# A state-space layer's tables moved from GpSimd to VectorE, its recurrence regrouped into two equal chains, its state products cut into quarter tiles

## The chip, the core and the metric

The program runs on one core of one Trainium2 chip. The core has five engines with a queue each: TensorE (PE in the profile; its weight loads are PEld), VectorE (DVE), ScalarE (ACT), GpSimd (POOL) and SyncE (SP, which here only issues DMAs). The engines run side by side and wait for each other by semaphores; a queue is worked off in order, so that an instruction that waits holds up all behind it. The metric is the device time of one execution in microseconds (us), lower is better.

## What is computed

A two-layer model on 256 tokens of width 2048, all in 32-bit floats. Layer 0 is a complex diagonal state-space mixer (S5: 128 groups of 16 channels with 64 complex states each) with a gated linear unit (GLU), then a SwiGLU feed-forward block; layer 1 is dilated-window attention and a second feed-forward block. The change is in the mixer alone:

```python
lb = exp(lam * dt)                         # complex, 128 x 64
bb = ((lb - 1) / lam) * b                  # 128 x 64 x 16
h[t] = lb * h[t-1] + bb @ u[t]             # 256 tokens, by groups
y[t] = real(c @ h[t]) + d_skip * u[t]
g = gelu(y);  val, gate = split(g @ w_glu) # 2048 x 4096
x = x + val * sigmoid(gate)
```

## The kernel before

**The mixer in blocks of four tokens.** The 256 tokens are 64 blocks of four. With the powers of `lb` up to the fourth (`pf1` to `pf4`, made by `power`), a block's input to the state is a sum of four tap matrices (`taps`, tile `gp`), the state from block to block is a recurrence with `pf4`, and the output of a block is a local product within the block (`y_local`, with the matrices `mt`) plus a product of the state with powers times `c` (`y_state`, with the tables `fd`, made by `powers`). Partitions hold two groups of 64 states; the 64 group pairs are cut into four quarters `qr` of 16. One half (32 pairs) shares an input tile `ub` and a state tile `st`.

**A quarter's steps.** `gain` scales `b` (one product); `taps` are six pairs of a 128x512 product (`gpr`) and a 128x256 sum; `taps_T` transposes them on TensorE in four groups, each copied by ScalarE to `gt`; `inject` multiplies them with the inputs in four groups, each copied by ScalarE into the state tile (two copies). `build_c` makes `cp` (two pairs of product and sum), `build_m` multiplies the taps with masked copies of `cp` (`cb`) on TensorE, and `store_m`, `finish_m` and six small DMAs make `mt` of it. `powers` are eight more pairs of product and sum. `spread` makes masked copies `fbd` of `fd` on ScalarE, 16 instructions a quarter.

**Who does what.** VectorE makes the parameters, the first quarter's taps, `build_c` of two quarters and the recurrence; GpSimd makes `gain`, the other taps, the other `build_c`, all `powers` and `finish_m`. `InOrder` (T, A, G, W for TensorE, ScalarE, GpSimd, VectorE) keeps these instructions in the order of the code; nearly all carry the line of its helper (L65), so the rows are read by tile names. Small tables (`NA`, `NP`, `NC`, `NH_`, ...) say how many steps of the recurrence go between other work.

**The recurrence** is 63 steps of three VectorE instructions: a product (tile `spr`), a sum (`ssm`), and an addition into the state (tile `actr`, the shared name of all big activation tiles). Before it is cut into chains `a` (quarter 0), `b` (quarters 1 and 2) and `c` (quarter 3), and steps of two chains alternate.

**The GLU** follows quarter by quarter: `y_state`, then Gelu (`gm`), four transposes for each half of the quarter (`y_T`), a hi copy by ScalarE and a lo difference by VectorE (`actt`), and then the weights' products. Each weight chunk (1 MB, four rows of 128) is split in two halves into `whi` (ScalarE) and `wlo` (VectorE); a row of weights gives six matmuls of 128x512. The first gate and the first value block, 16 rows of weights each, are fed side by side, as soon as a quarter of the mixer's output is there; the other six of the eight blocks follow (`block`, lines 128 to 130). After the GLU the kernel is such blocks to its end.

```python
def run(n, *its):
    for _ in range(n):
        for it in its:
            op = next(it, None)
            ...
order = [(blk, nb, c) for c in range(4) for blk, nb in ((0, 4), (1, 0))]
```

Of the kernel before, what the change touches and what calls it, by code (L numbers as in the profile page):

```python
# [15 lines left out]
ALU = mybir.AluOpType  # L16
# [31 lines left out]
NP = 39  # L48
NL = 0
NC = 7  # L50
NG_ = (6, 8, 11, 15)
NA = 54
NY = 11
NH_ = ((15, 11, 11, 18), (12, 12, 12, 12), (15, 15, 27, 15), (0, 0, 0, 0))
SPN = (6, 6, 4, 0)
# [12 lines left out]
class Net:  # L68
# [141 lines left out]
    def s5_glu(self):  # L210
# [8 lines left out]
        nc.sync.dma_start(out=spp, in_=io["sp"])  # L219
        pairs = early.tile([P, P], FP32, name="pairs")  # L220
        nc.sync.dma_start(out=pairs, in_=io["pairs"])
        for q in range(2):
            nc.sync.dma_start(out=xc[:, 16 * q:16 * q + 16], in_=io["x_c"][:, 16 * q:16 * q + 16])
        masks = late.tile([P, 2], FP32, name="masks")
        nc.sync.dma_start(out=masks, in_=io["masks"])
        nc.sync.dma_start(out=self.ident, in_=io["ident"])

# [35 lines left out]
        state = {0: (sts[0], 0), 1: (sts[1], 0), 2: (sts[1], 16), 3: (sts[0], 16)}  # L263

        gps = {}
        def gain(qr):
            bt = early.tile([P, 2, 16, GI], FP32, name="bt", tag="bt", bufs=1)
            nc.sync.dma_start(out=bt, in_=io["b"][:, :, 16 * qr:16 * qr + 16])
            gb = early.tile([P, 16, GI], FP32, name="gb", bufs=2)
            nc.sync.dma_start(out=gb, in_=io["gain_b"][:, 16 * qr:16 * qr + 16])  # L270
            if qr < 2:
                g = early.tile([P, 2, 16, 4, GI], FP32, name="gp", tag="gp", bufs=2)
            else:
                g = self.xres.tile([P, 2, 16, 4, GI], FP32, name="gp", tag="xr")
            tt(g[:, :, :, 3], bt, gb.unsqueeze(1).broadcast_to([P, 2, 16, GI]), ALU.mult, G)
            gps[qr] = g

        def c_load(qr):
            ct = late.tile([P, 2, 16, GI], FP32, name="ct", tag="fd", bufs=4)
            nc.sync.dma_start(out=ct, in_=io["c"][:, :, 16 * qr:16 * qr + 16])  # L280
            return ct

        gain(0)
        cts = {qr: c_load(qr) for qr in range(4)}
        ds = late.tile([P, 2, 64], FP32, name="ds")
        dmask = late.tile([P, GI], FP32, name="dmask")
        nc.sync.dma_start(out=ds, in_=io["dsk"])
        nc.sync.dma_start(out=dmask, in_=io["dmask"])
# [44 lines left out]
        def form(nm, z, eng=V):  # L333
            f = late.tile([P, 2, 2, 64], FP32, name=nm)
            eng.tensor_copy(out=f[:, 0, 0], in_=z[:, 0])
            eng.tensor_copy(out=f[:, 1, 1], in_=z[:, 0])
            eng.tensor_copy(out=f[:, 1, 0], in_=z[:, 1])
            eng.tensor_scalar(out=f[:, 0, 1], in0=z[:, 1], scalar1=-1.0, scalar2=None, op0=ALU.mult)
            return f

        def cmul(out, f, z, eng=V):
            pr = early.tile([P, 2, 2, 64], FP32, name="pr", tag="gprv", bufs=1)
            tt(pr, f, z.unsqueeze(1).broadcast_to([P, 2, 2, 64]), ALU.mult, eng)
            tt(out, pr[:, :, 0], pr[:, :, 1], ALU.add, eng)

        pf = [form("pf1", lam, W)]
# [4 lines left out]
        def power(eng=V):  # L351
            k = len(pf) + 1
            z = early.tile([P, 2, 64], FP32, name=f"pw{k}")
            cmul(z, pf[0], pw[-1], eng)
            pw.append(z)
            pf.append(form(f"pf{k}", z, eng))

        power(W)
        power(W)
# [19 lines left out]
        gts = {}  # L379

        def taps(qr, eng, nm):
# [125 lines left out]
        def run(n, *its):  # L507
            for _ in range(n):
                for it in its:
                    op = next(it, None)  # L510
                    if op is not None:
                        op()
# [494 lines left out]
```

## Time and profile before

| | us |
|---|---|
| median of 3 runs (2507.66 to 2507.81) | 2507.7 |
| profiled execution, first to last instruction | 2504.1 |
| TensorE busy | 2391.9 |
| VectorE busy | 1411.4 |
| ScalarE busy | 1106.7 |
| GpSimd busy | 162.4 |
| two of eight GLU blocks done at | 253.9 |

Times in the trace are counted from its first instruction; the time of a run has 3.6 us more than the profiled span (2507.7 less 2504.1). Busy time of TensorE tells little in the first 250 us, because its matmuls are short there and overlap; what matters is when it waits, and for whom.

### The profile page before, as it was taken

The numbers are of one execution on the slowest core, as the hardware profiler recorded it, in microseconds if no ns is written. First come the engines' busy times: TensorE is split into PE (matmuls) and PEld (weight loads), VectorE is DVE, ScalarE is ACT, GpSimd is POOL, SyncE is SP. The second block draws the span as 40 slices with busy tenths as digits, with TensorE's granted clock in tenths as the row PEclk, the third lists the DMA queues.
The fourth block names the chain that finished last, engine by engine and source line by source line (L and its number), as shares of the span: only waits on it lengthen the run. The fifth ranks groups of instructions, "written<-read, shape, count | busy, mean of one in ns | idle before, by whom it ended". The sixth has DMA issues, their size and how long they took to land.

```text
span 2504.1 us, 28310 instructions
## 1 busy us (share of the span) xinstructions
PE 2391.9 (96%) x11200; PEld 1935.8 (77%) x11200; DVE 1411.4 (56%) x2098; ACT 1106.7 (44%) x1423; POOL 162.4 (6%) x156
## 2 busy tenths in 40 slices
PE   5439999999999999999999999999999999999999
PEld 5427888888888888888888888878888888888887
DVE  9997545445444444555545667765444444454444
ACT  6316444444433444445444555545444433344433
POOL 7911000000000000000000100100000000000000
PEclk8569999999999999999999999999999999999999
DMA  3103555555555555555555444445555555555554
GB/s 115 63 1 120 185 186 185 184 186 183 185 187 189 186 185 181 182 185 194 185 185 172 165 154 149 152 151 178 180 185 182 185 185 190 192 185 179 186 194 148
DMA packets 64949, 423.50 MB, mean 169 GB/s; under 512 B 8240, under 2 KB 12208, under 8 KB 14384
## 3 DMA queue, kind: packets, MB, share of 16 engines
q1 hardware_dynamic: 63664, 419.60, 49.2%
q8 instruction: 87, 1.43, 0.2%
q10 hardware_dynamic: 1152, 2.10, 0.2%
q14 instruction: 46, 0.38, 0.0%
HBM read 418.79 MB, written 2.10 MB: 168 GB/s over the span
## 4 chain that ended last, share of the span: by engine, by line
PE 91%; DVE 8%; issue 0%; ACT 0%; POOL 0%; DMA 0%; POOLq 0%
PE mm L128 29%; PE mm L130 29%; PE mm L129 29%; DVE actr L65 2%; DVE spra L65 1%; DVE ssma L65 1%; PE mm L65 1%; PE ms L847 1%; PE tr L733 1%; DVE sprb L65 1%; PE tr L798 1%; DVE ssmb L65 1%; DVE sprc L65 1%; DVE gpr L65 0%; PE tr L847 0%; PE tr L191 0%
## 5 line engine op out<-in xcount | busy, mean ns | idle before, releaser
L110 DVE TENSOR_TENSOR wlo<-raw,whi 128x1024 fp32r<-128x1024 f32 x768 | 939.2, 1225 | 991.6 <-ACT whi L109 990.2
L109 ACT CAST whi<-raw 128x1024 fp32r<-128x1024 f32 x768 | 804.6, 1048 | 1147.8 <-PE mm L130 1130.5
L128 PE MATMUL mm<-whi,actt 128*128 128x512 f32 x3072 | 1221.3, 398 | 1.1 <-ACT whi L109 1.1
L130 PE MATMUL mm<-whi,actt 128*128 128x512 f32 x3072 | 1215.0, 396 | 0.0
L129 PE MATMUL mm<-wlo,actt 128*128 128x512 f32 x3072 | 1214.8, 395 | 0.0
L130 PEld LDWEIGHTS mm<-whi,actt 128*128 128x128 f32 x3072 | 575.9, 187 | 138.6
L128 PEld LDWEIGHTS mm<-whi,actt 128*128 128x128 f32 x3072 | 576.0, 188 | 137.7 <-ACT whi L109 1.6
L129 PEld LDWEIGHTS mm<-wlo,actt 128*128 128x128 f32 x3072 | 576.0, 187 | 136.6
L65 PE MATMUL mm<-fbd,actr 128*64 128x128 f32 x64 | 6.3, 382 | 66.5 <-DVE actr L65 66.5
L180 POOL TENSOR_TENSOR r<-m,mhalf 128x1 f32<-128x1 f32 x6 | 3.2, 552 | 995.0 <-DVE m L179 848.9
L785 POOL TENSOR_TENSOR sc<-ssq,mhalf 128x8 f32<-128x8 f32 x16 | 32.1, 2005 | 475.0 <-DVE ssq L783 475.0
L65 PEld LDWEIGHTS mm<-fbd,actr 128*64 128x64 f32 x64 | 6.2, 233 | 66.6 <-issue 66.6
L65 PE MATMUL mm<-whi,actt 128*128 128x512 f32 x128 | 47.0, 435 | 7.2 <-DVE actt L65 6.9
L719 ACT ACTIVATE sg<-mm,r 128x512 f32<-128x512 f32 x44 | 30.1, 689 | 21.3 <-PE mm L130 21.1
L65 PEld LDWEIGHTS mm<-whi,actt 128*128 128x128 f32 x128 | 25.8, 204 | 14.9 <-DVE actt L65 8.3
L856 ACT ACTIVATE s<-s,mx 128x384 f32<-128x384 f32 (+1 forms) x32 | 24.8, 774 | 25.2 <-DVE mx L854 25.2
L65 POOL TENSOR_TENSOR fpr<-pf,cp 128x512 f32<-128x512 f32 x32 | 34.6, 1080 | 2.3
L65 ACT ACTIVATE gm<-mm 128x512 f32<-128x512 f32 x2 | 1.2, 598 | 70.0 <-PE mm L65 70.0
L723 DVE SCALAR_TENSOR_TENSOR sg<-mm,r,sg 128x512 f32<-128x512 f32 x44 | 30.9, 744 | 0.0
L65 DVE TENSOR_TENSOR spra<-pf,actr 128x64 f32<-128x64 f32 x63 | 30.4, 482 | 0.6
L65 DVE TENSOR_TENSOR ssma<-spra 128x32 f32<-128x32 f32 x63 | 29.3, 465 | 0.5
L781 ACT ACTIVATE sq<-mm 128x512 f32<-128x512 f32 x32 | 19.0, 593 | 23.5 <-PE mm L130 23.5
(190 smaller groups left out, 1243.7 us busy)
## 6 DMA issues: line engine op xcount, KB each, us to landing
raw<-w_gu SPq DMA_DIRECT2D x176, 1024.0 KB, 4.8
raw<-w_down SPq DMA_DIRECT2D x88, 1024.0 KB, 4.9
raw<-w_q SPq DMA_DIRECT2D x48, 1024.0 KB, 4.9
raw<-w_kv SPq DMA_DIRECT2D x32, 1024.0 KB, 4.9
raw<-w_glu SPq DMA_DIRECT2D x30, 1024.0 KB, 4.9
raw<-w_o SPq DMA_DIRECT2D x16, 1024.0 KB, 4.9
actr<-x_c SPq DMA_DIRECT2D x2, 1024.0 KB, 6.1
actr<-w_glu SPq DMA_DIRECT2D x2, 1024.0 KB, 7.1
```

What stands on the lines that cost most here:

```text
L65: return lambda *a, **k: self.tc.keep_in_program_order(call(*a, **k))
L109: (scalar or self.nc.scalar).copy(out=hi, in_=r)
L110: (vector or self.nc.vector).tensor_tensor(out=lo, in0=r, in1=hi.bitcast(FP32), op=ALU.subtract)
L128: matmul(ps[th], lhsT=a[:, 0, ts], rhs=hi, start=(k == 0), stop=False)
L129: matmul(ps[th], lhsT=a[:, 0, ts], rhs=lo, start=False, stop=False)
L130: matmul(ps[th], lhsT=a[:, 1, ts], rhs=hi, start=False, stop=(k == n - 1))
L719: nc.scalar.activation(out=s, in_=ps[th], func=AF.Silu, scale=rs[th])
L723: nc.vector.scalar_tensor_tensor(out=sg[th], in0=ps[th], scalar=rs[th], in1=sg[th], op0=ALU.mult, op1=ALU.mult)
L733: nc.tensor.transpose(out=pt[:, k, th * P:(th + 1) * P], in_=sg[th][:, c:c + P], identity=self.ident)
L785: nc.gpsimd.tensor_tensor(out=sc, in0=ssq, in1=self.mhalf.rearrange("p (a b) -> p a b", a=2), op=ALU.pow)
L798: nc.tensor.transpose(out=pt[:, hh, th * P:(th + 1) * P], in_=ns[th][:, 2 * hp + hh], identity=self.ident)
L847: nc.tensor.matmul(pss[g], lhsT=q[g][:, th * P:(th + 1) * P], rhs=kT[:, h, 0:n], start=True, stop=True)
```

## The change

Everything lies in the function of layer 0.

- VectorE makes all tables: `gain`, `taps`, `build_c` and `powers` of all quarters. GpSimd keeps the memsets, one product `dsm` (128x1024) at the start and the power for the norm.
- `taps_T` and `inject` become one function, `taps_inject`: a group's transposes, its copy, its products and its copies stand behind each other before the next group's.
- `store_m` adds `dsm` on VectorE; the copy on ScalarE and GpSimd's addition go.
- The tables stand ahead of the recurrence, which is two chains of equal width (32 pairs each), run alternately to their end with nothing between. The small tables of numbers go.
- `spread` goes. `y_state` reads `fd` itself in quarter tiles: 64 rows by 64 columns of the array, 64 matmuls of 64 columns a quarter instead of 32 of 128.
- In the GLU only the first gate block is fed beside the mixer's output; the first value block is an ordinary block behind it. The early load of the first two weight chunks goes; all weight splits' differences are on VectorE (four of 16 halves were on GpSimd).
- `b`, `gain_b` and `c` are loaded whole at the start.

```diff
-        def taps(qr, eng, nm):
+        def pair(out, f, src):
+            pr = early.tile([P, 2, 16, GI], FP32, name="gpr", bufs=2)
+            yield lambda: tt(pr, f.unsqueeze(3).broadcast_to([P, 2, 16, GI]), src, ALU.mult, W)
+            yield lambda: tt(out, pr[:, 0], pr[:, 1], ALU.add, W)
+
+        def taps(qr):
             mo = 16 * qr
             g = gps[qr]
...
-        def taps_T(qr):
-            g = gps[qr]
-            gts[qr] = []
+        def taps_inject(qr):
+            g, st, mo = gps[qr], sts[qr // 2], 16 * (qr % 2)
             for j2 in range(4):
                 gtt = early.tile([P, 2, 2, P], FP32, name="gt", tag="gt", bufs=4)
-                gts[qr].append(gtt)
                 ps = self.ps_tr.tile([P, 2, 2, P], FP32, name="tr")
...
                 A.copy(out=gtt, in_=ps)
-
-        def inject(qr):
-            st, mo = state[qr]
-            for j2 in range(4):
                 ps = self.ps_mm.tile([P, 2, 2, 2, NS], FP32, name="mm")
...
-                A.copy(out=mt[r, 3, mo:mo + 16].rearrange("p (j y) o -> p j y o", y=2), in_=ps[r, :, :, xx])
...
+                tt(mt[r, 3, mo:mo + 16].rearrange("p (j y) o -> p j y o", y=2), ps[r, :, :, xx],
+                   dsm[r, mo:mo + 16].rearrange("p (j y) o -> p j y o", y=2), ALU.add, W)
...
-        def y_state(qr, j4, ps):
-            st, mo = state[qr]
-            for j in range(4):
+        def y_state(qr, pss):
+            st, mo = sts[qr // 2], 16 * (qr % 2)
+            for jq in range(8):
                 for ri in range(2):
                     for xx in range(2):
-                        mq = 2 * (4 * j4 + j) + xx
-                        T.matmul(ps[64 * xx:64 * xx + 64, j],
-                                 lhsT=st[:, 0:64, ri, mo + mq],
-                                 rhs=fb[qr][j4][:, :, ri, :, mq - 8 * j4].rearrange("p y t o -> p t y o"),
-                                 start=False, stop=(ri == 1), skip_group_check=True)
...
+                        for y in range(2):
+                            r = slice(64 * y, 64 * y + 64)
+                            T.matmul(pss[y][64 * xx:64 * xx + 64, jq],
+                                     lhsT=st[r, 0:64, ri, mo + 2 * jq + xx],
+                                     rhs=fds[qr][r, :, ri, 2 * jq + xx],
+                                     start=False, stop=(ri == 1), skip_group_check=True)
...
+        run(taps(0))
+        taps_inject(0)
+        power()
         gain(2)
-        taps(2, G, "g")
...
+        gain(3)
+        run(taps(1), coefs())
+        taps_inject(1)
         build_u(1)
...
+        run(taps(2))
+        taps_inject(2)
+        run(taps(3))
+        taps_inject(3)
+        fd = self.act_raw([P, 2, 4, 2, 16, GI])
+        fds = {0: fd[:, 0], 1: fd[:, 1]}
+        run(*[build_c(qr) for qr in range(2)])
+        run(*[build_c(qr) for qr in range(2, 4)])
         ms = {}
         for qr in range(4):
...
+            ms[qr] = build_m(qr)
+            if qr > 1:
+                fds[qr] = self.xres.tile([P, 4, 2, 16, GI], FP32, name="fdx", tag="xr")
+            run(powers(qr))
             if qr:
                 store_m(qr - 1, ms[qr - 1])
...
+        run(scan("a", 0), scan("b", 1))
...
+        prepare(0)
+        y_state(0, yl[0])
+        gms = {0: gelu(yl[0])}
+        y_state(1, yl[1])
...
+        y_T(0, gms[0])
+        gms[1] = gelu(yl[1])
+        gb0 = self.open_block(KT)
+        for c in range(4):
+            if c + 1 < 4:
+                prepare(c + 1)
+            for w in ws.pop(c):
+                self.products(gb0, w, lhs, T)
+            if c < 2:
+                yl[c + 2] = y_local(c + 2, self.ps_ms, "ms")
+                y_state(c + 2, yl[c + 2])
+                gms[c + 2] = gelu(yl[c + 2])
+            if c == 1:
+                gtile[1] = self.act_tile()
+                lhs += [gtile[1][:, k] for k in range(8)]
+            if c < 3:
+                y_T(c + 1, gms[c + 1])
```

The first place is TensorE's queue behind the first inputs `ub` (transposes that read `ident` and `actr`). `tr<-ident,gp` are the transposes of the taps, `mm<-actr,gt` their products with the inputs. Before:

```order
L65 MATMUL tr<-ident,gp 128x128 x16
L65 MATMUL mm<-actr,gt 64x128 x32
L65 MATMUL tr<-ident,gp 128x128 x16
L65 MATMUL tr<-ident,actr 128x64 x16
L65 MATMUL ms<-ident,actr 128x64 x16
L65 MATMUL mm<-actr,gt 64x128 x32
```

And now:

```order
L57 MATMUL tr<-ident,gp_230 128x128 x4
L57 MATMUL mm<-actr,gt 64x128 x8
L57 MATMUL tr<-ident,gp_230 128x128 x4
L57 MATMUL mm<-actr,gt 64x128 x8
L57 MATMUL tr<-ident,gp_230 128x128 x4
L57 MATMUL mm<-actr,gt 64x128 x8
L57 MATMUL tr<-ident,gp_230 128x128 x4
L57 MATMUL mm<-actr,gt 64x128 x8
```

A quarter's sixteen transposes stood ahead of its products; now each group of four is followed by the products that need its copy, and the next group's transposes stand behind these.

The second place is VectorE's queue where the third quarter's powers begin (`fdx` is their table, in the buffer that held the third quarter's taps; `actr<-ms,dsm` is `store_m` of the first quarter). Before, VectorE has recurrence steps and `build_c` at the corresponding place, and GpSimd the powers:

```order
L65 TENSOR_TENSOR spra<-pf_290,actr 128x64
L65 TENSOR_TENSOR gpr<-cform,ct 128x512 [waits DMAHW1_49,DVE_49]
L65 TENSOR_TENSOR ssma<-spra 128x32 [waits DVE_49]
L65 TENSOR_TENSOR cp<-gpr 128x256 [waits DVE_49]
L65 TENSOR_TENSOR actr<-actr,ssma 128x2x16 [waits DVE_49,Activation_49]
```

And now:

```order
L57 TENSOR_TENSOR actr<-ms,dsm 64x256 [waits PE_49,Pool_49]
L57 TENSOR_TENSOR actr<-ms,dsm 64x256
L57 TENSOR_TENSOR gpr<-pf_223,cp 128x512
L57 TENSOR_TENSOR fdx<-gpr 128x256 [waits DVE_49,PE_49]
L57 TENSOR_TENSOR gpr<-pf_223,cp 128x512
L57 TENSOR_TENSOR fdx<-gpr 128x256 [waits DVE_49]
```

VectorE has two waits for TensorE here that it did not have: `store_m` for the first `build_m`, and the first write of `fdx` for the third, which reads the taps in that buffer. The same stands once more for the fourth quarter, and the recurrence is behind both.

The third place is TensorE's queue where the recurrence ends. `ms<-actr` and `mm<-actr` are local and then state products, `tr<-ident,gm` the transposes of Gelu's result. Before:

```order
L65 MATMUL mm<-actr 64x4x16 x32
L65 MATMUL mm<-fbd,actr 64x128 x32
L65 MATMUL ms<-actr 64x4x16 x32
L65 MATMUL tr<-ident,gm 128x128 x8
L65 MATMUL mm<-whi,actt 128x512
```

And now:

```order
L57 MATMUL ms<-actr 64x64 x32
L57 MATMUL mm<-actr 64x64 x32
L57 MATMUL ms<-actr 64x64 x64
L57 MATMUL mm<-actr 64x64 x64
L57 MATMUL tr<-ident,gm 128x128 x8
L57 MATMUL mm<-whi,actt 128x512
```

Two quarters' state products, of twice as many matmuls at half the width, now stand ahead of the first weights' product; the last two of the four stand between the first block's quarters.

## Rows read from the trace of the kernel before

**Rows 1.** Page: span, busy time, forty slices of VectorE and the granted clock.

```profile
span 2504.1 us, 28310 instructions
...
DVE  9997545445444444555545667765444444454444
...
PEclk8569999999999999999999999999999999999999
```

**Rows 2.** Busy time by stretch: us, then busy us and count by engine, granted clock.

```profile
137.50:161.00 23.50, 0.03 (x2) 0.06 (x2) 23.50 (x167) 0.00 (x0) 0.07 (x1) 0.50 0.00 1
...
254.00:300.00 46.00, 46.00 (x203) 37.13 (x202) 23.86 (x26) 21.05 (x27) 0.00 (x0) 1.00 0.54 183
```

**Rows 3.** Timeline (start, us) of VectorE: a product beside GpSimd, a product and a sum without it.

```profile
27.60 1.43 DVE L65 TENSOR_TENSOR gpr<-pf,gp 128x512 f32<-128x512 f32 x1
...
50.59 0.68 DVE L65 TENSOR_TENSOR gpr<-cform,ct 128x512 f32<-128x512 f32 x1
...
51.86 0.41 DVE L65 TENSOR_TENSOR cp<-gpr 128x256 f32<-128x256 f32 x1
```

**Rows 4.** Timeline of VectorE: one step of chains a and b with GpSimd idle.

```profile
139.36 0.28 DVE L65 TENSOR_TENSOR sprb<-pf,actr 128x128 f32<-128x128 f32 x1
139.56 0.18 DVE L65 TENSOR_TENSOR ssma<-spra 128x32 f32<-128x32 f32 x1
139.68 0.22 DVE L65 TENSOR_TENSOR ssmb<-sprb 128x64 f32<-128x64 f32 x1
139.82 0.18 DVE L65 TENSOR_TENSOR actr<-actr,ssma 128x32 f32<-128x32 f32 x1
```

**Rows 5.** Timeline of TensorE and ScalarE: inputs' copies, products with the taps, copies behind them.

```profile
22.30 2.41 ACT L65 ACTIVATE actr<-ms,masks 128x512 f32<-128x512 f32 x4
...
33.42 4.93 PE L65 MATMUL mm<-actr,gt 128*64 128x128 f32 x64
...
35.45 1.05 ACT L65 COPY actr<-mm 128x252 f32<-128x252 f32 x2 [1.33 <-PE mm L65]
...
51.58 1.08 ACT L65 COPY gt<-tr 128x512 f32<-128x512 f32 x2 [0.32 <-PE tr L65]
...
51.90 3.71 PE L65 MATMUL mm<-actr,gt 128*64 128x128 f32 x64
...
53.04 3.71 ACT L65 COPY actr<-mm 128x252 f32<-128x252 f32 x8 [0.39 <-PE mm L65]
```

**Rows 6.** Timeline: TensorE's `build_m`, masked copies, and GpSimd's product with the skip weights.

```profile
56.53 1.70 ACT L65 ACTIVATE cb<-cp,masks 128x256 f32<-128x256 f32 x4
57.49 4.96 PE L65 MATMUL ms<-cb,gp 128*128 128x64 f32 x32 [1.87 <-ACT cb L65]
...
71.85 19.26 PE L65 MATMUL ms<-cb,gp 128*128 128x64 f32 x96 [1.86 <-ACT cb L65]
...
84.06 0.62 POOL L65 TENSOR_TENSOR dsm<-ds,dmask 128x256 f32<-128x256 f32 x1
```

**Rows 7.** Timeline of TensorE: a quarter's local products, then a quarter's state products.

```profile
167.06 2.10 PE L65 MATMUL ms<-actr 128*64 128x64 f32 x64
...
189.52 4.99 PE L65 MATMUL ms<-fbd,actr 128*64 128x128 f32 x64
```

**Rows 8.** Timeline: Gelu, and the hi and lo copies of the mixer's output.

```profile
236.84 0.61 ACT L65 ACTIVATE gm<-ms 128x512 f32<-128x512 f32 x1 [3.21 <-PE ms L65]
...
240.99 0.61 ACT L65 CAST actt<-tr 128x256 fp32r<-128x256 f32 x1 [1.43 <-PE tr L65]
241.63 0.63 DVE L65 TENSOR_TENSOR actt<-tr,actt 128x256 fp32r<-128x256 f32 x1 [5.22 <-ACT actt L65]
```

**Rows 9.** The chain that ended last: transposes two GLU blocks apart.

```profile
256.59 0.66 PE tr L191 x6
302.06 0.65 PE tr L191 x6
```

**Rows 10.** Busy time by stretch (columns of rows 2), TensorE after a wait.

```profile
185.20:190.00 4.80, 4.75 (x17) 3.37 (x19) 4.29 (x19) 4.80 (x12) 0.00 (x0) 0.64 0.01 2
```

More of the change, by code (lines that the diff above doesn't have):

```diff
@@ L223, in s5_glu @@
             nc.sync.dma_start(out=xc[:, 16 * q:16 * q + 16], in_=io["x_c"][:, 16 * q:16 * q + 16])
+        bt = early.tile([P, 2, 64, GI], FP32, name="bt")
+        gb = early.tile([P, 64, GI], FP32, name="gb")
+        nc.sync.dma_start(out=gb, in_=io["gain_b"])
+        for q in range(2):
+            nc.sync.dma_start(out=bt[:, :, 32 * q:32 * q + 32], in_=io["b"][:, :, 32 * q:32 * q + 32])
         masks = late.tile([P, 2], FP32, name="masks")
@@ L262, in s5_glu @@
             G.memset(st[:, 0], 0.0)
[L263 to L288, printed above, removed]
+        dsm = late.tile([P, 64, GI], FP32, name="dsm")
+        tt(ds[:, 0], ds[:, 0], ds[:, 1], ALU.mult, G)
+        tt(dsm, ds[:, 0].unsqueeze(2).broadcast_to([P, 64, GI]),
+           dmask.unsqueeze(1).broadcast_to([P, 64, GI]), ALU.mult, G)
         ssc = early.tile([P, 2, 4], FP32, name="ssc")
@@ L463, in m_operand, with build_m @@
             return cb
-        def build_m(qr, cbs):
+        def build_m(qr):
+            cbs = [m_operand(qr, j4) for j4 in range(2)]
             ps = self.ps_ms.tile([P, 8, 2, 2, GI], FP32, name="ms")
@@ L504, in scan, with run @@
+                yield lambda: tt(v, v, sm, ALU.add, W)
             for c in range(63):
                 yield from step(c)
-        def run(n, *its):
-            for _ in range(n):
-                for it in its:
+        def run(*its):
+            its = list(its)
+            while its:
+                for it in list(its):
                     op = next(it, None)
-                    if op is not None:
+                    if op is None:
+                        its.remove(it)
+                    else:
@@ L512, in run, with powers @@
                         op()
         fds = {}
-        def powers(qr, eng, nm):
+        def powers(qr):
             mo = 16 * qr
-            if qr < 2:
-                fds[qr] = [late.tile([P, 2, 16, GI], FP32, name="fd", tag="fd", bufs=4) for _ in range(4)]
-            else:
-                buf = self.xres.tile([P, 4, 2, 16, GI], FP32, name="fdx", tag="xr")
-                fds[qr] = [buf[:, t] for t in range(4)]
             for t in range(4):
                 for k in range(2):
-                    yield from cmulb(fds[qr][t][:, k], pf[t][:, :, k, mo:mo + 16], cp[:, :, mo:mo + 16], nm, eng)
@@ L579, in s5_glu @@
             scale_x(h)
[L580 to L581 removed]
         build_u(0)
[L583 to L585 removed]
+        run(taps(0))
+        taps_inject(0)
+        power()
         gain(2)
[L587 to L595 removed]
@@ L648, in s5_glu, with prepare @@
-        for i in range(2):
-            prepare(i)
-        run(NL, sa, sb)
-        gms = [y_state(0, j4, yl[0][j4]) for j4 in range(2)]
-        run(NP, sb, sc)
-        yl[1] = [y_local(1, j4, self.ps_ms, "ms") for j4 in range(2)]
+        yl = {0: y_local(0, self.ps_ms, "ms"), 1: y_local(1, self.ps_mm, "mm")}
+        run(scan("a", 0), scan("b", 1))
+        ws = {}
+        def prepare(c):
+            raw = self.load_chunk(io["w_glu"][4, c])
+            ws[c] = [self.split(raw, half, A, W) for half in range(2)]
@@ L697, in s5_glu @@
                     sg.append(s)
-                ps = vb0[0] if nb == 0 else self.block([io["w_glu"][nb, c] for c in range(4)], lhs)
+                ps = self.block([io["w_glu"][nb, c] for c in range(4)], lhs)
                 for th in range(2):
```

224 lines of the change are left out of this document (64 added, 160 removed).

## The prediction

> **What bounds the kernel now.** I read the page first: span, slices, clock [rows 1]. The span is 2504.1 us; VectorE is about half busy after the first three slices (62.6 us each), and the clock of TensorE is low only in the first three. So the change can matter only there. Then busy time by stretch [rows 2]: from 254 to 300 us TensorE is busy all 46.00 us at a granted clock of 1.00, while in the recurrence's last stretch (137.5 to 161) it does 0.03 us of work in 23.50 and VectorE is busy all of them. The chain that ended last [rows 9] shows the same transposes at 256.59 and 302.06: two GLU blocks take 302.06 - 256.59 = 45.47 us, so a block of 16 rows is 22.7 with its transposes, 22.4 without (1.40 a row). From 253.9, when two of the eight GLU blocks are done, the kernel is bound by TensorE and the change touches nothing but weight splits. If E is the time at which the changed kernel has its first gate and first value block done, then
>
> time after = 2507.7 + (E - 253.9).
>
> The profiled span is 2504.1 and the median 2507.7, 3.6 more outside the span, in both kernels alike. So the whole question is E.
>
> What sets 253.9 now is VectorE and GpSimd. A 128x512 product takes 1.43 us on VectorE while GpSimd works and 0.68 alone [rows 3]: the two hold each other up. The recurrence is drawn out by that, and the tables by GpSimd; then products and GLU follow.
>
> **The change part by part: from the start to the injections.** ScalarE's copies of the inputs end at 22.30 + 2.41 = 24.7 [rows 5]. `dsm` now stands on GpSimd at the start, beside VectorE's parameters: four products of 0.62 [rows 6] hold up VectorE by 0 to 2.5; I take 1.2, the middle, and 25.9.
>
> `taps_inject` makes a ping-pong of what was a pipeline. A group is four transposes, their copy (1.08 for two, 0.54 one), eight products and two copies; the next transposes stand behind the products, and the next products wait for the copy of these transposes, which stands behind the copies of the last group on ScalarE. One round: from the products' start to the first copy 53.04 - 51.90 = 1.14 at full clock and 35.45 - 33.42 = 2.03 early; two copies 3.71 / 8 x 2 = 0.93 less overlap, 0.85; then `gt` 0.54 and two hand-overs of 0.05 [rows 5]: 2.6 at full clock, 3.6 at low. Sixteen rounds of 2.6 are 41.6; `build_u` of the second half, two input sets' copies on ScalarE, 4.8 (twice 2.41); and four rounds at low clock, as one quarter's injection in the early row, 4.0. 25.9 + 41.6 + 4.8 + 4.0 = 76.3. Bounds: none at low clock 72.3, all sixteen 88.
>
> VectorE's tables cost the same span: 24 pairs of `taps`, 8 of `build_c`, 16 of `powers` at about 1.05 (0.68 + 0.41 less overlap, [rows 3]) are 50.4, of which six pairs of `powers` or more come behind the waits below. It is ready at about 72.7 and waits a little for TensorE; neither hides much more of the other.
>
> **Tables behind the injections.** One masked copy of `cb` (1.70 for four, two needed to start, 0.9) to 77.2. A `build_m` takes 4.96 when TensorE has just been quick and 19.26 / 3 = 6.42 in a row [rows 6]. VectorE's first write of `fdx` must wait for the third `build_m` (it reads the taps in that buffer): 77.2 + 5.0 + 6.4 + 6.4 + 0.5 = 95.5. Eight pairs of powers, the first product already made: 7.7, and a `store_m`, 1.2 by two sums of 0.41 and start-up: 104.4. Only then is the buffer for the fourth `build_m` free: 6.4 + 0.5, 111.3; again 7.7 and two `store_m` of 1.15: 121.3. There the recurrence begins.
>
> **Recurrence.** Starts of one step's instructions lie 0.20 (product), 0.14 and 0.14 apart for the 64-wide chain [rows 4]; both chains now have that size or nearly: 2 x 0.48 = 0.96, x 63 = 60.5. T0 = 181.8. GpSimd is idle, so the product's own time holds.
>
> **From T0 to E.** At T0 the local products and weight splits are done; 60 us cover the loads and the first four splits. On the path: state products of two quarters, 2Y; two Gelu sets, each four of 0.61 less overlap (0.4) plus a hi cast and hand-over of 0.7 [rows 8], 2.3 each, 4.6; first transposes and cast 0.65 + 0.62 = 1.3 [rows 8, 9]; gate block 22.4; the lo difference (0.63) late twice, 1.2; two local products of 2.10 [rows 7] between the gate's quarters, 4.2; state products of the other two quarters, 2Y; 2.0 for the last quarter's transposes, which stand behind a split of the next chunk on ScalarE; value block 22.4. Sum 58.1 + 4Y. The clock: after a wait TensorE gets 0.64 over the next 4.8 us [rows 10], so of the 12 us or so in short pieces before full rate a third is lost: 4, between 0 and 8.
>
> Y, the state products of one quarter, is what no row shows: quarter tiles of 64 rows by 64 columns, 64 matmuls (128 records) of 64 columns. Nearest rows [rows 7]: the local products, two column halves of full depth, 64 records in 2.10; the old state products, 64 records of twice the columns in 4.99. If all four tiles run at once at the pace of the first, Y is 128 / 64 x 2.10 / 2 = 2.1; if only two do, at the pace of the second, 2 x 4.99 = 10.0. I take 5.0: four at once at the second pace, which has the same state read as weights with a large step.
>
> The Trainium skill has a rule on this (TensorEngine Tiling (Array Packing), Key Properties): different tiles can load weights and multiply in parallel, and 64x64 gives four independent tiles. By it Y would be 2.1, and the time that of the third rival below; the trace shows only pairs of column halves, never row halves, so it neither agrees nor differs.
>
> E = 181.8 + 58.1 + 20.0 + 4 = 263.9, 10.0 later than now: 2517.7, 2518 rounded.
>
> **Costed at nothing.** `spread` goes from ScalarE, which waits in the tables anyway. Loads of weights are hidden by the recurrence's 60 us; without that cover each would be about 5. The splits' differences on VectorE are idle time after T0 where the blocks leave VectorE 23.86 us busy of 46 [rows 2]. If the last transposes did not stand behind a split, 2.0 less.
>
> **Rivals.** Within 0.2% (5.0 us) a measurement of this kernel can hardly be told from no change.
>
> 1. The state products run two at a time, Y = 10: E is 20 later, 2538. For it: the old ones took 0.156 a matmul for 0.066 in the local ones, with the strided read as the difference besides the columns. Against it: some overlap between row halves would already halve it.
> 2. TensorE stays at low clock through all injections, as the early row has 2.03 for 1.14: sixteen rounds of 3.6, 12 more, 2530. For it: the second slice has 0.5 [rows 1], and in the ping-pong TensorE waits half the time. Against it: products of the same kind got 1.14.
> 3. Four tiles at once, Y = 2.1: 4 x 2.9 less, E = 252.3, 2506: same.
> 4. The other side, faster: TensorE keeps its upper clock level through tables and tail. Rounds of 2.6 (72.3), each `build_m` half of 6.42, 3.2, no clock term: 72.3 + 0.9 + 9.6 + 0.5 = 83.3, + 8.9 = 92.2, + 3.7 + 10.0 = 105.9, + 60.5 = 166.4, + 78.1 = 244.5: 2498. It decides as soon as E is below 248.9. For it: 1.14 a round [rows 5] at full level. Against it: `build_m` took 6.42 though nothing else ran on TensorE [rows 6].
>
> **How the numbers follow.** Main forecast 0.43, with its own range 2510 to 2530 (clock 0 to 8, injections 72.3 to 80, `dsm` 0 to 2.5). Rival 1: 0.15. Rival 2: 0.12. Rival 3: 0.14. Rival 4: 0.16. Slower is the main one and rivals 1 and 2, less 0.03 for the edge of the main one's range near 5 us: 0.67. Same is rival 3, that edge, and a piece of rival 4 given up by half a clock: 0.16. Faster: 0.17, rival 4 with a small part of 3 in which the quick tiles meet a quick clock. The range must reach rival 4's edge and rival 1: 2497 to 2540; outside lie the sums of two bad cases, and of 3 with 4 (2486).
>
> **What would show it.** In the changed profile: injections of 2.6 us a group with TensorE waiting for `gt` and ScalarE for `mm`, ending near 76; VectorE's first `fdx` sum waiting for `ms` until 95; the recurrence from 121 to 182 at 0.96 a step, nothing on GpSimd; two state groups of about 5 us; no wait for a DMA; E at 264 and 1.40 a row behind. What would make it wrong: the injections run faster than by ping-pong, a third wait in the tables, state products outside 2 to 10, or waits for splits in the value block, which now has nothing beside it.

## The result, and the profile after

| | before | after |
|---|---|---|
| median (6 runs each) | 2507.68 us | 2519.96 us |
| lowest to highest | 2506.06 to 2507.88 | 2512.98 to 2526.01 |
| ratio, 95% interval | | 1.0049, 1.0032 to 1.0065 |
| profiled span | 2504.1 us | 2516.4 us |

The change makes the kernel slower, by 12.3 us in the medians; 2518 was forecast, within 2497 to 2540. The runs of the changed kernel lie 13 us apart, those of before 1.8: something in it varies. The profiled execution, at 2518.62, is near the median.

The page of the changed kernel, its span and the forty slices of VectorE and of the granted clock, as in [rows 1]:

```profile
span 2516.4 us, 28535 instructions
...
DVE  9493554544544444455544677765545444444444
...
PEclk7559999999999999999999999999999999999999
```

VectorE is less than half busy in the second slice (62.9 to 125.8 us), although it now makes all tables. So it waits there, and the timeline shows for whom. First TensorE and ScalarE, from the last copies of the inputs to the fourth quarter's products (start, us, engine, instruction; in brackets the idle time before it and what ended it):

```profile
23.24 2.40 ACT L57 ACTIVATE actr<-ms,masks 128x512 f32<-128x512 f32 x4
...
30.06 1.98 PE L57 MATMUL mm<-actr,gt 128*64 128x128 f32 x16 [0.67 <-ACT gt L57]
31.97 1.12 PE L57 MATMUL tr<-ident,gp 128*128 128x128 f32 x4
32.08 1.04 ACT L57 COPY actr<-mm 128x252 f32<-128x252 f32 x2 [2.07 <-PE mm L57]
33.12 0.58 ACT L57 COPY gt<-tr 128x512 f32<-128x512 f32 x1
33.76 1.97 PE L57 MATMUL mm<-actr,gt 128*64 128x128 f32 x16 [0.68 <-ACT gt L57]
...
75.71 1.09 PE L57 MATMUL mm<-actr,gt 128*64 128x128 f32 x16 [0.73 <-ACT gt L57]
...
78.34 1.09 PE L57 MATMUL mm<-actr,gt 128*64 128x128 f32 x16 [0.95 <-ACT gt L57]
...
80.97 1.09 PE L57 MATMUL mm<-actr,gt 128*64 128x128 f32 x16 [0.95 <-ACT gt L57]
82.11 1.00 ACT L57 COPY actr<-mm 128x252 f32<-128x252 f32 x2 [1.19 <-PE mm L57]
```

The ping-pong stands there as forecast: each engine's bracket names the other. It has two paces. At the lower clock level (granted 0.50 from 30.1 to 41.1 us) a group takes 33.76 - 30.06 = 3.70 us, at the upper one (1.00 from 75.7 to 82.0) 78.34 - 75.71 = 2.63. Of the sixteen groups nine ran at the lower one, six at the upper one, and in one it changed. The last products end at 82.06, the last copies at 83.11.

TensorE's `build_m` behind this, two quarters together and two alone, then VectorE's waits for them and the start of the recurrence (`spra`):

```profile
83.86 12.45 PE L57 MATMUL ms<-cb,gp 128*128 128x64 f32 x64 [1.79 <-ACT cb L57]
96.10 7.03 PE L57 MATMUL ms<-cb,gpx 128*128 128x64 f32 x32
112.06 7.06 PE L57 MATMUL ms<-cb,gpx 128*128 128x64 f32 x32 [8.93 <-DVE actr L57]
```

```profile
89.59 0.88 DVE L57 TENSOR_TENSOR actr<-ms,dsm 64x256 f32<-64x256 f32 x2 [17.01 <-PE ms L57]
...
103.18 0.42 DVE L57 TENSOR_TENSOR fdx<-gpr 128x256 f32<-128x256 f32 x1 [11.98 <-PE ms L57]
...
119.16 0.42 DVE L57 TENSOR_TENSOR fdx<-gpr 128x256 f32<-128x256 f32 x1 [6.52 <-PE ms L57]
...
128.84 0.29 DVE L57 TENSOR_TENSOR spra<-pf,actr 128x128 f32<-128x128 f32 x1
```

These are the three waits for `build_m`: 17.01, 11.98 and 6.52 us, 35.5 together. The first begins at 72.6, so that more than half of it is a wait for the injections to end. The recurrence ends at 188.5 (59.7 us, 0.95 a step). TensorE behind it; `ms` and `mm` are the state products of the first two quarters, then come those of the third with its local products ahead and transposes behind:

```profile
188.59 4.95 PE L57 MATMUL ms<-actr 64*64 64x64 f32 x128 [53.85 <-DVE actr L57]
193.19 4.92 PE L57 MATMUL mm<-actr 64*64 64x64 f32 x128
...
205.38 2.08 PE L57 MATMUL ms<-actr 128*64 128x64 f32 x64
207.39 4.91 PE L57 MATMUL ms<-fdx,actr 64*64 64x64 f32 x128
212.23 1.09 PE L57 MATMUL tr<-ident,gm 128*128 128x128 f32 x8
214.18 0.50 PE L57 MATMUL mm<-whi,actt 128*128 128x512 f32 x1 [0.85 <-ACT actt L57]
```

A quarter's state products (64 matmuls, which leave 128 records in the trace) take 4.9 us at both ends of the tail, for the 5.0 of the sum. The kernel before took 4.99 [rows 7]: the quarter tiles by themselves saved TensorE nothing. From the first weights' products on TensorE has gaps of less than 1 us only. The chain that ended last, where the two blocks are behind it, answers to [rows 9]:

```profile
267.02 0.66 PE tr L183 x6
312.70 0.66 PE tr L183 x6
```

267.02 - 256.59 = 10.4: by that E is 253.9 + 10.4 = 264.3, for the 263.9 of the forecast. The spans differ by 12.3; the other 1.9 come up behind, 1.4 of it at one place in the second layer, which the change does not touch. The kernel before scatters as much by itself: its spans on record go from 2503.9 to 2506.8, and the profiled one, 2504.1, is among the shortest. A run lasts 1.7 to 3.0 longer than its own span in every kernel here (2518.62 - 2516.4 = 2.2 in this one). The 3.6 given above for the kernel before is no such difference: it sets one short span against the median of other executions.

### The profile page after: what moved, and what is told of

It is laid out like the page before. It is cut to its first block, busy times and chain, and to the rows that moved or that the text cites. A ratio compares the mean times of both kernels' runs of the same rounds, so it can differ in the third digit from the quotient of the medians.

```text
span 2516.4 us, 28535 instructions
## 1 busy us (share of the span) xinstructions
PE 2403.2 (96%) x11456; PEld 1945.1 (77%) x11456; DVE 1361.6 (54%) x2033; ACT 1080.2 (43%) x1359; POOL 41.8 (2%) x33
## 4 chain that ended last, share of the span: by engine, by line
PE 93%; DVE 3%; ACT 0%; issue 0%; POOL 0%; POOLq 0%
PE mm L120 29%; PE mm L122 29%; PE mm L121 29%; PE ms L57 2%; PE mm L57 1%; PE ms L770 1%; DVE actr L57 1%; PE tr L656 1%; PE tr L721 1%; DVE sprb L57 1%; DVE spra L57 1%; PE tr L770 0%; PE tr L183 0%; DVE gpr L57 0%; DVE ssmb L57 0%; DVE ssma L57 0%
## 5 line engine op out<-in xcount | busy, mean ns | idle before, releaser
L121 PE MATMUL mm<-wlo,actt 128*128 128x512 f32 x3104 | 1229.5, 396 | 0.0
L57 PE MATMUL ms<-actr 128*64 128x64 f32 (+1 forms) x320 | 13.1, 292 | 63.2 <-DVE actr L57 54.2
L57 PEld LDWEIGHTS ms<-actr 128*64 128x64 f32 (+1 forms) x320 | 12.3, 198 | 64.4 <-issue 64.4
L57 PE MATMUL mm<-actr,gt 128*64 128x128 f32 x256 | 25.7, 365 | 14.9 <-ACT gt L57 14.9
L642 ACT ACTIVATE sg<-mm,r 128x512 f32<-128x512 f32 x44 | 30.1, 689 | 21.3 <-PE mm L122 21.0
L57 PEld LDWEIGHTS mm<-actr,gt 128*64 128x64 f32 x256 | 20.3, 187 | 20.5 <-ACT gt L57 20.5
L784 DVE SCALAR_TENSOR_TENSOR p<-s,z,p 128x128 f32<-128x128 f32 (+1 forms) x64 | 26.3, 411 | 3.8 <-ACT p L782 3.6
L57 ACT COPY actr<-mm 128x252 f32<-128x252 f32 x32 | 16.5, 620 | 27.3 <-PE mm L57 27.3
L660 DVE TENSOR_TENSOR actt<-tr,actt 128x512 fp32r<-128x512 f32 x44 | 28.2, 682 | 0.0
L659 ACT CAST actt<-tr 128x512 fp32r<-128x512 f32 x44 | 23.6, 590 | 10.1 <-PE tr L656 10.1
```

What stands on the lines that cost most here:

```text
L57: return lambda *a, **k: self.tc.keep_in_program_order(call(*a, **k))
L121: matmul(ps[th], lhsT=a[:, 0, ts], rhs=lo, start=False, stop=False)
L642: nc.scalar.activation(out=s, in_=ps[th], func=AF.Silu, scale=rs[th])
L660: nc.vector.tensor_tensor(out=ht[:, k0:k0 + 2, 1], in0=pt, in1=ht[:, k0:k0 + 2, 0].bitcast(FP32), op=ALU.subtract)
L784: nc.vector.scalar_tensor_tensor(out=pr, in0=sc[:, g], scalar=z, in1=pr, op0=ALU.mult, op1=ALU.add)
```

## The experiments

Two theories stood at the start. **A**: the loss lies in front of the recurrence, in the ping-pong of the injections and in the waits for `build_m`. **B**: it lies behind it, in the quarter-tile state products and the value block on its own. Each kernel below is the changed one with the edit shown. Medians are compared with the kernel before on the same chip: 2507.7 for the first four, 2506.8 for the next four, 2507.7 for the ninth, 2506.4 for the last three.

**1. Transposes first.** The old order within a quarter.

```diff
+            gts = []
             for j2 in range(4):
...
                 A.copy(out=gtt, in_=ps)
+                gts.append(gtt)
+            for j2 in range(4):
+                gtt = gts[j2]
                 ps = self.ps_mm.tile([P, 2, 2, 2, NS], FP32, name="mm")
```

> Changed kernel with each quarter's sixteen transposes ahead of its products again, nothing else. Theory A (the loss sits in front of the recurrence, in the ping-pong of injections and in the waits for build_m): the injections, which end at 83 us in the changed kernel, end at about 72 (between 62 if TensorE gets its upper clock level, 25.7 + 28.0 + 4.8 and a few, and 80 if it stays at the lower one, 25.7 + 49.6 + 4.8); everything behind comes that much earlier, about 11 us: 2509. Theory B (the loss sits behind the recurrence, in the quarter-tile state products and the value block on its own): the injections end earlier too, but the total stays near 2520.

Measured: 2497.07 (2496.62 to 2497.88), ratio 0.9962 (0.9947 to 0.9977). That is 22.9 less than the changed kernel, and 10.7 less than before. TensorE and VectorE:

```profile
28.02 3.71 PE L57 MATMUL mm<-actr,gt 128*64 128x128 f32 x64
...
57.12 3.71 PE L57 MATMUL mm<-actr,gt 128*64 128x128 f32 x64
...
62.72 11.63 PE L57 MATMUL ms<-cb,gp 128*128 128x64 f32 x64 [1.88 <-ACT cb L57]
...
81.21 0.42 DVE L57 TENSOR_TENSOR fdx<-gpr 128x256 f32<-128x256 f32 x1 [7.14 <-PE ms L57]
...
106.87 0.29 DVE L57 TENSOR_TENSOR spra<-pf,actr 128x128 f32<-128x128 f32 x1
```

In three of four quarters the products take 3.71, which is the figure of [rows 5] at the upper level (4.57 in the other). The injections end at 60.8, 21.2 earlier, and the recurrence starts 22.0 earlier, at 106.87. Theory A holds; I had expected only half of it, since I took an end of 72 from between the two levels. The spread of the runs is gone too.

**2. A buffer of its own** for the third quarter's `fdx`.

```diff
...
-                gtt = early.tile([P, 2, 2, P], FP32, name="gt", tag="gt", bufs=4)
+                gtt = early.tile([P, 2, 2, P], FP32, name="gt", tag="gt", bufs=3)
...
-                fds[qr] = self.xres.tile([P, 4, 2, 16, GI], FP32, name="fdx", tag="xr")
+                fds[qr] = (late.tile([P, 4, 2, 16, GI], FP32, name="fd2") if qr == 2 else
+                           self.xres.tile([P, 4, 2, 16, GI], FP32, name="fdx", tag="xr"))
```

> Changed kernel with the third quarter's powers table in a buffer of its own, the fourth's in the one that held the third's taps, and three instead of four copies of gt. Theory A: VectorE's powers of the third quarter run in the time in which it waited for build_m, those of the fourth start at about 103; the recurrence starts at about 113.5 in place of 128.8, so 15 us less: 2505. Theory B: VectorE waits elsewhere or TensorE is late behind the recurrence anyway: near 2520.

Measured: 2500.07 (2493.16 to 2509.23, 10 runs), 0.9973 (0.9959 to 0.9987). The wait of 11.98 is gone and that of 6.52 has become 2.47:

```profile
96.43 0.43 DVE L57 TENSOR_TENSOR fdx<-gpr 128x256 f32<-128x256 f32 x1 [2.47 <-PE ms L57]
...
106.11 0.29 DVE L57 TENSOR_TENSOR spra<-pf,actr 128x128 f32<-128x128 f32 x1
```

But the profiled execution had only three groups of injections at the lower level, and its last products ended at 74.9, not 82.1. From there to the recurrence it took 31.2, for 128.84 - 82.06 = 46.8 in the changed kernel: the edit is worth 15.5, the rest is the other clock.

**3. `store_m` early**, by order alone.

```diff
-            run(powers(qr))
-            if qr:
+            if qr > 1:
                 store_m(qr - 1, ms[qr - 1])
+            run(powers(qr))
+            if qr == 1:
+                store_m(0, ms[0])
```

> Changed kernel with the second and third store_m ahead of the powers that stood before them, an order alone. Theory A: the second store_m frees its PSUM buffer at about 97 in place of 112, so that the fourth build_m follows the third without the 8.9 us gap on TensorE; VectorE still waits for the third (103) but no more for the fourth: about 7 us less, 2513. Theory B: near 2520.

Measured: 2506.91 (2503.82 to 2513.82, 10 runs), 0.9998 (0.9989 to 1.0008). The third and fourth `build_m` now run in one piece, and the recurrence starts at 123.15:

```profile
97.74 13.86 PE L57 MATMUL ms<-cb,gpx 128*128 128x64 f32 x64
...
123.15 0.29 DVE L57 TENSOR_TENSOR spra<-pf,actr 128x128 f32<-128x128 f32 x1
```

The profiled execution had ten groups at the lower level and ended its injections at 82.5, much like the changed kernel's; the two recurrences start 5.7 apart and the two times, 2513.82 and 2518.62, differ by 4.8. The medians differ by 13, which the order alone does not explain; this was the slowest of its ten runs.

**4. Row halves apart.** Neighbours in TensorE's queue share the row half.

```diff
-            for jq in range(8):
-                for ri in range(2):
-                    for xx in range(2):
-                        for y in range(2):
+            for y in range(2):
+                for jq in range(8):
+                    for ri in range(2):
+                        for xx in range(2):
```

> Changed kernel with the state products of one row half ahead of those of the other, so that neighbours in TensorE's queue differ in the column half alone. If quarter tiles of different rows now run at once, a quarter's state products (4.9 us) take up to 9.8, four times 4.9 more: 2539. If only column halves ran at once, or if the queue's own pace sets 38 ns a record, they stay at 4.9 and the time near 2520.

Measured: 2539.62 (2530.83 to 2543.99), 1.0120 (1.0096 to 1.0143).

```profile
195.82 8.59 PE L57 MATMUL ms<-actr 64*64 64x64 f32 x122 [53.41 <-DVE actr L57]
...
223.36 9.11 PE L57 MATMUL ms<-fdx,actr 64*64 64x64 f32 x128
```

38 ns a record become 71. So in the changed kernel tiles of different row halves do run at once. The Trainium skill (TensorEngine Tiling (Array Packing), Key Properties) says that different tiles can load weights and multiply in parallel; these rows agree. The total fits the expectation partly by chance: this execution had fifteen groups of injections at the lower level.

**5. The waits filled.** Does the ping-pong cost what it costs because of the clock? Four products that nobody reads stand where TensorE waited.

```diff
                 A.copy(out=gtt, in_=ps)
+                self.warm(4, self.ident, T)
                 ps = self.ps_mm.tile([P, 2, 2, 2, NS], FP32, name="mm")
```

> Changed kernel, in each group of the injections four products of the identity that nobody reads stand between the transposes and the products, where TensorE waited 0.7 to 1.0 us for the copy. The changed kernel had 10 of 16 groups at 3.75 us with the granted clock at 0.50 and the others at 2.63 with 1.00. Theory C (the price of the ping-pong is mostly the lower clock level, given because TensorE waits): with the waits filled all groups but the first few take 2.63, the injections end at 72 to 74, not at 83, the time is near 2509 and its runs lie closer together. Rival (the level has another cause, or the added products delay the others): groups stay at 3.75 or grow, 2520 to 2535.

Measured: 2511.83 (2509.17 to 2514.28, 10 runs), 1.0018 (1.0008 to 1.0027): 8.1 less than the changed kernel, with more work. Fifteen of the sixteen groups ran at the upper level. The busy times by stretch over the injections, columns as in [rows 2], of the changed kernel:

```profile
24.00:83.00 59.00, 42.35 (x352) 32.11 (x351) 47.28 (x109) 31.16 (x60) 0.00 (x0) 0.68 0.00 1
```

of the fourth kernel:

```profile
24.00:89.00 65.00, 51.18 (x352) 39.20 (x351) 47.26 (x109) 31.89 (x60) 0.00 (x0) 0.52 0.00 1
```

and of this one:

```profile
24.00:74.00 50.00, 45.03 (x480) 38.66 (x479) 47.27 (x109) 29.65 (x59) 0.00 (x0) 0.97 0.01 2
```

The same 352 records of TensorE (here with 128 added) take 65, 59 or 50 us as the granted clock is 0.52, 0.68 or 0.97. This is what scatters the changed kernel's runs: its two shortest (2512.98 and 2513.58) had a mean granted clock of 0.976 and 0.975, its two longest (2525.93 and 2526.01) 0.966, and the ten runs of this edit lie 5.1 us apart in place of 13. The last products of this execution:

```profile
72.26 1.09 PE L57 MATMUL mm<-actr,gt 128*64 128x128 f32 x16
```

They end at 73.35, 8.7 earlier than in the changed kernel, but still 12.5 later than in experiment 1 (60.83). So the clock is the smaller part of what the ping-pong costs, and theory C's "mostly" does not hold; the larger part is that the two engines work in turn.

**6. Edits 1 and 2 together.**

> Transposes first and own buffer together. Theory A: VectorE has its tables without a wait of more than 1 us; from 72.5 on two store_m, 16 pairs at 1.06, and two more store_m: the recurrence starts at about 93, 14 us earlier than with the transposes first alone: 2484. Theory B (behind the recurrence something else, loads or splits, is late by then): not below 2492.

Measured: 2483.73 (2482.35 to 2484.66), 0.9907 (0.9893 to 0.9922). VectorE's longest wait in the tables is now 0.34:

```profile
83.93 0.42 DVE L57 TENSOR_TENSOR fdx<-gpr 128x256 f32<-128x256 f32 x1 [0.34 <-PE ms L57]
...
93.61 0.29 DVE L57 TENSOR_TENSOR spra<-pf,actr 128x128 f32<-128x128 f32 x1
```

Theory B falls: with the front put right, the same tail gives a kernel 23 us faster than before. What the new tail costs or gives against the old one is not shown by this.

**7. Powers of two quarters on GpSimd**, on top of edit 1.

```diff
...
-            run(powers(qr))
+            run(powers(qr, *([G, "gpg"] if qr > 1 else [])))
```

> Transposes first, and the powers of the third and fourth quarter back on GpSimd, which undoes a third of the tables' move; VectorE goes from store_m straight to the recurrence, at about 90. Theory D (what the move buys is that VectorE and GpSimd no longer hold each other up): while GpSimd makes its 16 pairs (2.0 us each, up to about 113) a step of both chains takes 2.5 to 3.5 us in place of 0.95, and the recurrence ends at about 165, as with VectorE making them (166.5): 2494 to 2500. Rival (they don't hold each other up here): the recurrence ends at 150: 2481.

Measured: 2494.14 (2493.63 to 2494.85), 0.9950 (0.9935 to 0.9964). VectorE's step of both chains beside GpSimd:

```profile
92.36 0.81 DVE L57 TENSOR_TENSOR spra<-pf,actr 128x128 f32<-128x128 f32 x1
93.09 1.14 DVE L57 TENSOR_TENSOR sprb<-pf,actr 128x128 f32<-128x128 f32 x1
...
96.11 0.81 DVE L57 TENSOR_TENSOR spra<-pf,actr 128x128 f32<-128x128 f32 x1
```

A step takes 96.11 - 92.36 = 3.75 in place of 0.95; the recurrence starts 18 us earlier than in experiment 1 and ends 2.4 earlier, at 164.1. Theory D holds: GpSimd's help costs nearly what it gives. It does not cost more, though: the total is 2 to 3 us below experiment 1, so this run does not show that the move of these powers to VectorE gained anything.

**8. Half the columns** in the state products, on top of edit 1; this leaves out the state's part for two of four tokens.

```diff
-                            T.matmul(pss[y][64 * xx:64 * xx + 64, jq],
+                            T.matmul(pss[y][64 * xx:64 * xx + 64, jq, 0:2],
...
-                                     rhs=fds[qr][r, :, ri, 2 * jq + xx],
+                                     rhs=fds[qr][r, 0:2, ri, 2 * jq + xx],
```

> Transposes first, and the state products with 32 of their 64 columns (the output lacks the state's part for two of four tokens of a block). If the columns set their pace, a quarter takes about 2.5 us in place of 4.9 and the total is 9 to 10 lower than with the transposes first alone: 2487. If the loads of the 64-column weights or the queue set it (38 ns a record), it stays at 4.9: 2497.

Measured: 2499.25 (2497.16 to 2500.36), 0.9968 (0.9956 to 0.9979).

```profile
188.10 4.87 PE L57 MATMUL ms<-fdx,actr 64*64 64x32 f32 x128
```

Half the columns, the same 4.9: the columns do not set the pace. The total is even 2.2 above experiment 1; in this execution the state products already began 2.3 later (168.95 for 166.61), and behind the recurrence three sets of transposes took 1.6 to 2.0 instead of 1.1.

**9. Time innermost.** On top of experiment 6 the state tile is laid out so that the weights of the state products have a step of one element instead of 64.

```diff
-        sts = [self.act_raw([P, NS, 2, 32]) for _ in range(2)]
+        sts = [self.act_raw([P, 2, 32, NS]).rearrange("p r m c -> p c r m") for _ in range(2)]
```

> Both edits of the fastest version so far, and the state tile laid out with time innermost, so that TensorE reads the weights of the state products in one piece instead of with a step of 64 elements, and VectorE's recurrence takes the step instead. If the step sets the 38 ns a record, a quarter's state products fall from 4.9 to 2.1 to 2.6 us, four times 2.3 to 2.8 less: 2473, if the recurrence keeps 0.95 a step. If the queue or the weight load itself sets it: 4.9 and 2484. If VectorE pays for the step, the recurrence's steps grow from 0.95, by 0.63 us in all for each 0.01.

Measured: 2492.91 (2492.48 to 2494.22), 0.9941 (0.9925 to 0.9958).

```profile
94.72 0.38 DVE L57 TENSOR_TENSOR spra<-pf,actr 128x128 f32<-128x128 f32 x1
...
95.96 0.39 DVE L57 TENSOR_TENSOR spra<-pf,actr 128x128 f32<-128x128 f32 x1
...
184.44 2.09 PE L57 MATMUL ms<-fd,actr 64*64 64x64 f32 x128
```

Both things happen at once. The step of the weights' read set the pace: without it a quarter takes 2.09, the lower bound of the forecast. But VectorE now pays: 95.96 - 94.72 = 1.24 for this step, 1.21 in the mean, for 0.95; over 63 steps that is 16, and the products give only about 6.6, since the first quarter's took 3.53 at the lower level and a pause of 3.19 stands in the last one's.

**10 to 12. Two, four or eight states side by side.** Between the two layouts; here the line for two (with four it is `[P, 2, 8, NS, 4]`, with eight `[P, 2, 4, NS, 8]`), with the recurrence, the copies and the weights indexed to match.

```diff
-        sts = [self.act_raw([P, NS, 2, 32]) for _ in range(2)]
+        sts = [self.act_raw([P, 2, 16, NS, 2]) for _ in range(2)]
...
```

> Both edits of the fastest version so far, and a state tile in which two states stand side by side and then the time: TensorE's weights have a step of 2 elements in place of 64 (64 elements: 4.9 us a quarter, 1 element: 2.1), VectorE's recurrence runs of 2 elements in place of 32 or 64 (a step of 0.95 us) or 1 (1.21). If both prices lie between in proportion to the logarithm of the step, a quarter is 2.6 and a step 1.15: 2483.7 - 9 + 12.6 = 2487. If VectorE's price is by single elements alone and TensorE's step of 2 costs nothing, 2473; the other way round 2500.

> The same with four states side by side: weights with a step of 4 elements, runs of 4 for VectorE. In proportion to the logarithm a quarter is 3.0 and a step 1.10: 2483.7 - 7.6 + 9.5 = 2486. If a step as small as this is free for TensorE and a run of 4 for VectorE, 2473.

> The same with eight states side by side: weights with a step of 8 elements (32 bytes), runs of 8 for VectorE. In proportion to the logarithm a quarter is 3.5 and a step 1.06: 2483.7 - 5.6 + 6.9 = 2485. If 8 in a run are enough for VectorE and 32 bytes is small enough for TensorE, 2473; if neither, 2500.

Measured: with two 2478.06 (2477.43 to 2478.76), 0.9885 (0.9871 to 0.9900); with four 2480.61 (2478.95 to 2483.45), 0.9897 (0.9882 to 0.9911); with eight 2480.00 (2478.96 to 2482.94), 0.9895 (0.9879 to 0.9912). With two, the recurrence and the third quarter's products:

```profile
94.54 0.29 DVE L57 TENSOR_TENSOR spra<-pf,actr 128x128 f32<-128x128 f32 x1
...
95.49 0.29 DVE L57 TENSOR_TENSOR spra<-pf,actr 128x128 f32<-128x128 f32 x1
...
168.50 2.15 PE L57 MATMUL ms<-fd,actr 64*64 64x64 f32 x128
...
185.63 0.70 PE L57 MATMUL ms<-fdx,actr 64*64 64x64 f32 x15 [3.15 <-issue]
```

with four, the same products:

```profile
171.27 4.07 PE L57 MATMUL ms<-fd,actr 64*64 64x64 f32 x128
```

The prices are not in proportion to the logarithm, they are steps: a pair of elements costs VectorE nothing (0.95 a step), and TensorE next to nothing (2.15). Four and eight (4.07, and 4.09 with eight) bring back about 70% of TensorE's loss. The version with two is the fastest measured, 28.3 us below before. It gains 5.7 on experiment 6, not the 11 that 2.7 in each of four quarters would give: the first quarter's products still took 3.69 at the lower level, and 3.15 went in a pause in the last quarter's.

## Why the prediction was right

**The frame.** "So the whole question is E" held: E moved by 10.4 for a forecast of 10.0, and behind it the program kept its pace but for the 1.9 told above. A wrong step was to take 2507.7 and 253.9 as of one execution: 253.9 comes from one with a short span, and by the 1.7 to 3.0 that lie outside the span in the other runs, 3.6 is too much by 0.6 to 1.9. That the 1.9 behind E made up for it was luck.

**Start.** Copies of the inputs end at 25.64, forecast 25.9: right.

**Injections.** The mechanism was right, group by group: 2.63 and 3.70 measured for 2.6 and 3.6. The term that failed is the number of groups at the lower level: I took four, there were nine and a half. So they ended at 83.1 with the last copies, not at 76.3, 6.8 later. It lies between the main forecast and rival 2, which had all sixteen slow; experiment 4's execution, with fifteen, is that rival. That "products of the same kind got 1.14" was the wrong argument against it: in the old order TensorE did not wait between them.

**Waits in the tables.** Both `fdx` waits and the late fourth `build_m` came where they were put. From the end of the injections to the recurrence the sum had 121.3 - 76.3 = 45.0; it took 128.84 - 83.1 = 45.7. Experiments 2 and 3 take them away one by one. The wait of 17.01 for the first `build_m` is not named in the prediction, but its sum holds it, since it follows TensorE up to the third.

**Recurrence.** 60.5 forecast, 59.7 measured.

**Tail.** 188.5 to 264.3 is 75.8; the sum had 82.1. This is the second mis-sized part, 6.3 too long, and it offset the first, 6.8 too short: that E came within 0.4 is luck. The 4.6 for Gelu was too much: `gelu` of the first two quarters runs while TensorE works on, so that nothing of it is seen; that of the third and the fourth stands ahead of another quarter's cast on ScalarE and delays it by 0.4 to 0.6. The third's:

```profile
212.41 1.21 ACT L57 ACTIVATE gm<-ms 128x256 f32<-128x256 f32 x4 [7.06 <-PE ms L57]
213.49 0.64 ACT L57 CAST actt<-tr 128x256 fp32r<-128x256 f32 x1
```

The clock's 4 was too much, since the state products take 4.9 at either level (granted 0.50 in the first quarter's, 1.00 in the third's) and the weights' products start at the upper one. The 2.0 for the last quarter's transposes behind a split was 1.35 in all with their own time. In turn the transposes with their casts, that delay included, cost 1.8 to 2.0 a quarter between the gate's quarters (212.23 to 214.18), not 1.2 for two.

**State products.** Y was 4.9 for 5.0, and for the reason given: four tiles at once (experiment 4), slowed by the state's read with a large step (experiments 9 to 12), not by columns (experiment 8). Rival 1 (10) needed pairs only, rival 3 (2.1) a read without the step; experiment 9 gave just that. By the rule of the Trainium skill (TensorEngine Tiling (Array Packing), Key Properties) tiles run at once, and that held; the 2.1 that the prediction worked out from it came only with the weights close together.

**Rival 4**, the upper clock level through tables and tail, did not come: `build_m` took 6.2 to 7.1 us a quarter, at granted clocks of 0.50 to 0.57. Even in experiment 5, with the waits filled, the first two took 13.58 together. That it can be had for a while is shown by experiments 7 and 9, whose first two took 7.36 together at 1.00, and whose last two were back at 0.50.

**The answer to why the change loses.** Its other parts gain: with the old order of the injections alone it is 10.7 faster than before (experiment 1). Which of them gives how much is not shown: VectorE's steps are four times as quick without GpSimd beside it, but with the powers of two quarters put back on GpSimd the kernel is no slower (experiment 7). The ping-pong costs 22.9, by its order more than by the clock (experiment 5), and turns a gain into a loss. The buffer shared by `fdx` and the taps costs another 12 to 13 (experiment 6).

## What to carry to other kernels

Where two engines hand a tile to and fro, put the next tile's first half ahead of this one's second half; otherwise their times add up, and TensorE's pauses may cost its clock as well, so that the same code scatters from run to run. Before work is moved to a faster engine, look at which of its writes reuse a buffer that a slower one still reads: the gain can sit there whole. A layout that two engines read has a price on each side; a run of two 32-bit elements was cheap for both here.

## What the runs showed of the hardware

- **Row halves run at once.** 64x64 tiles of fp32 take 38 ns a record with row halves alternating and 71 with them apart (experiment 4). When the weights lie close, alternating ones take 16 to 17 at the upper clock level and 28 to 29 at the lower one (experiments 9 and 10).
- **The step of the weights' read.** At the upper clock level 128 records of 64-column weights took 2.09 us with a step of 4 bytes, 2.15 with 8, 4.07 with 16, 4.09 with 32 and 4.9 with 256. The Trainium skill (SBUF — State Buffer, Door 1: The DMA port swizzle) speaks of lines of 16 bytes in SBUF which need two accesses each for full bandwidth. The jump between 8 and 16 bytes agrees with that. The same passage allows a free stride of four fp32 elements; here a step of four doubled the time, and the measurement decides. What makes 256 bytes slower again is not shown.
- **VectorE** paid 0.26 us a step of six instructions for single elements 256 bytes apart, and nothing for pairs.
- **The clock.** Nearly the same stream of instructions was granted 0.52, 0.68 or 0.88 in the injections of different executions (65, 59 and 52 us), and 0.97 with the waits filled. Yet `build_m` ran at about 0.50 with TensorE busy throughout in most executions, and at 1.00 for its first two quarters in experiments 7 and 9; why was not settled.
- **A pause without a releaser** stands behind the 113th or 114th record of the last quarter's state products in nine of the profiled executions: 0.28 us in experiment 6, 0.60 in experiment 1, 3.15 with pairs. In all nine it ends about 2.3 us (2.2 to 2.4) after a packet of the DMA queue of kind `instruction` (q8, 16 KB), for instance 183.4 and 185.63 with pairs. In the changed kernel that packet came at 224.0, and the 113th record ended only at about 226.4: there is no pause. So TensorE probably waits for its next instructions there, and the quicker it gets to that place, the longer; no run tested this.
